# Pairing q, k blocks, moving DRAM copies and spreading branch loads in a one-layer encoder kernel

## The chip, the cores and the metric

The kernel runs on one core of a Trainium2 chip. The time is device microseconds of one launch; the number for a kernel is the median of its runs. A separate profiled execution gives the trace. Engines are called as in the profile: PE (TensorE, matmuls; PEld its weight loads), DVE (VectorE), ACT (ScalarE), POOL (GpSimd) and SP, whose queue issues most of the DMAs. Every engine takes its instructions in program order.

## The reference

One layer of a streaming encoder on x of 1024 tokens by 1024 features, all in f32:

```
h  = rmsnorm(x)
z  = h @ w_in                      # qa fa ia ga (4 x 512), qb kb vb (3 x 512), gate_a gate_b (2 x 1024)
oa = HGRN2(qa, fa, ia, ga)         # 4 heads of 128, chunk-wise linear recurrence
ob = BandAttn(qb, kb, vb)          # 8 heads of 64: q, k head-normalised; each chunk of 64 sees itself and 8 before it; bias by distance
x += (sigmoid(gate_a) * (oa @ w_branch_a) + sigmoid(gate_b) * (ob @ w_branch_b)) @ w_out
x += (silu(h2 @ w_gate) * (h2 @ w_up)) @ w_down          # h2 = rmsnorm(x)
x += sigmoid(h3 @ w_ple_gate) * (p @ w_ple_proj)         # h3 = rmsnorm(x)
```

## The kernel before

**Arithmetic.** Every f32 operand of a large matmul is split in two f32r parts: `hi`, a cast, and `lo = x - hi`. A product is three matmuls of 128x128 by 128x512 (hi hi, hi lo, lo hi). `gemm` issues them. A weight therefore costs a load into a raw tile, a cast on ACT and a subtraction on POOL before PE can use it.

**Order.** The program is written out as Python generators that are advanced in a fixed order, and `order` pins each engine to program order. A generator yields after a piece of work, usually six matmuls. `fetch` (L165) issues the load of the next weight of a planned list and appends a little generator to `self.later`; `tick` (L181) advances everything in `later` by one, so that the cast and subtraction of a weight are issued at the third tick after its fetch. The stream of q, k and branch work is wrapped in `ticked`, which ticks once per yield. There are four buffers for split weights (`RING`), two raw ones (`RAW`), 32 slots of 128x1024 f32 for everything large, and eight PSUM banks.

**Stages around the change.**
- *HGRN*: four heads, one after the other, in `hgrn_mix`. Seven levels per head (m = 1, 2, ..., 64) run mostly on DVE. They are woven with a fill of matmuls: two gate columns, then `attn_v` (v of the attention), then the first 20 yields of `attn_in`. At each level, and once more after the first output block, a head also calls `next(self.copies, None)`, which issues on SP one copy of 512 KB from a weight in DRAM to a scratch tile in DRAM. There are 32 of them (8 of w_out, 24 of w_down); later accumulating DMAs on POOL (`self.adds`) turn them into the sums of a Strassen product, one in each odd step of attention and more after it, first the eight of w_out.
- *q and k*: `attn_in` computes q, k for heads 0 to 3 and then 4 to 7 (`two`), eight blocks of 128 tokens each. Four weights, each two of eight feature chunks by 512 columns, make a set. `tokens` (L250) goes over the weights of a set and, for each, over the blocks of a group: one yield per weight and block. Here a group is a single block, 32 yields per set. The first group of a set takes its weights as they become ready (`lazy`); during the last block (b == 7) each of four yields fetches a weight of what comes next. `qk_norm` copies a block's q, k from PSUM to an SBUF tile, squares it into a second tile `sq`, and one tick later sums the squares on DVE, scales on POOL and, three ticks on, stores the block to DRAM.
- *attention*: `attention` runs 32 steps (pair of heads, block) and two more to drain, n = 0 to 33. For two = 0 the steps are blocks 0 to 7 with two pairs each (n = 0 to 15), then again for two = 1. Block b sees min(b + 1, 5) blocks of keys. A step takes two yields from `feed`, the rest of `attn_in` (44 yields; 4 ahead of step 0, done with step 19) and then `branch_a`. An even step loads the q, k block of the next even step (`qk_load`).
- *branch operands*: at the end of step 17 `keep_heads` stores the first two finished attention tiles, and `load_in(self.od)` loads the four HGRN outputs. `split_in` splits them (ACT cast, POOL subtraction) in steps 18, 19, 19 and 20 (`SPLITS`). `branch_a` (32 yields from step 20) multiplies them with four weights in turn, two output columns of blocks each, and gates the results; `branches` follows with the four weights of the other branch. `gate_load` loads two gate tiles per call.

The lines that are touched or followed: `FIRST` (L33), `hgrn_mix` (L526, L592), `attn_v` (L631), `qk_norm` (L650), `attn_in` (L669), `attention` (L808 to L850), `branch_a` (L1122), `branches` (L1147). The profile shows most instructions of DVE, ACT and POOL under L72, where a helper issues them, and all matmuls under L103 (transposes L106), so groups are told apart by tile names: `wr` raw weight, `wh` and `wl` its parts, `pm` a PSUM bank, `s` a slot, `m` a small tile, `d` a DRAM scratch tile.

Of the kernel before, what the change touches and what calls it, by code (L numbers as in the profile page):

```python
# [14 lines left out]
AF = mybir.ActivationFunctionType  # L15
# [15 lines left out]
SLOTS = 32  # L31
LATE = 8
FIRST = 5  # L33
RING = 4
RAW = 2
AHEAD = 3
# [38 lines left out]
class Trunk:  # L75
# [386 lines left out]
    def hgrn_mix(self, h):  # L462
# [26 lines left out]
        while m < P:  # L489
# [33 lines left out]
                    rows = slice(2 * m * j, 2 * m * j + m)  # L523
                    (self.V.tensor_copy if j == 0 else nc.scalar.copy)(av[rows, :, j, :], ps[rows, :8 * m].rearrange("p (c m) -> p c m", m=m))
            cur = nxt
            next(self.copies, None)  # L526
            if m == 2 and h < 3:
                next(more)
                self.head_load(h + 1)
# [97 lines left out]
    def attn_v(self):  # L627
        self.fetch()
        ws = []
        self.v = [self.slot() for _ in range(4)]  # L630
        for blks in ((0, 1), (2,), (3,), (4,), (5,), (6, 7)):  # L631
            pss = []
            for j, _ in enumerate(self.tokens(ws or self.lazy(ws), blks, pss)):
                if blks[0] == 0 and j == 1:
                    self.gate_keep()
                if blks[0] == 6 and j % 2:
                    self.fetch()
                yield 1296
            for b, ps in zip(blks, pss):
                for p in range(4):  # L640
                    self.nc.scalar.activation(self.v[p][:, b * P:b * P + P], ps[:, p * P:p * P + P], AF.Copy, scale=self.r[:, b:b + 1])
# [8 lines left out]
    def qk_norm(self, k, ps):  # L650

        late = self.stacks
        qk, sq = [self.small(HALF, tag="qk" if late else "bias", shape=(P, HALF if late else 640))[:, :HALF] for _ in range(2)]
        (self.V.tensor_copy if late else self.A.copy)(qk, ps)
        self.A.activation(sq, ps, AF.Square)
        yield
        ss = self.small(8)
        heads = lambda t: t.rearrange("p (a d) -> p a d", d=64)
        self.V.tensor_reduce(ss, heads(sq), axis=AX.X, op=ALU.add)
        b = k % 8  # L660
        self.V.tensor_scalar(ss, ss, 1.0 / 64, self.epsv[:, b:b + 1], ALU.mult, ALU.add)
        self.G.tensor_tensor(ss, ss, self.mhalf[:, 0:8], ALU.pow)
        self.G.tensor_tensor(heads(qk), heads(qk), ss[:, :].unsqueeze(2).to_broadcast([P, 8, 64]), ALU.mult)
        yield
        yield
        yield
        self.store(self.qk_at(k), qk)

    def attn_in(self):  # L669

        self.qkd = [self.spill() for _ in range(8)]
        for two in range(2):
            ws = []
            for b in range(8):
                pss = []
                for _ in self.tokens(ws or self.lazy(ws), (b,), pss):
                    if b == 7:
                        self.fetch()
                    yield 1296
                self.later.append(self.qk_norm(8 * two + b, pss[0]))  # L680

    def qk_load(self, k):
        if k < 16:
# [81 lines left out]
    def attention(self):  # L765
# [35 lines left out]
        for i in range(4):  # L801
# [3 lines left out]
            if i == 3:  # L805
                drain(stack(0))
                drain(self.hgrn_out())
        drain(self.copies)  # L808
        self.adds = chain(self.osum, self.wsum)
        while self.queue:  # L810
            self.rest()
# [2 lines left out]
        for n in range(whole + 2):  # L814
            if n % 2 and n < whole:
                next(self.adds)
            if n % 2 == 0:
                self.qk_load(n // 2 + 1)
            stage(n - 1, 1)
            next(feed, None)  # L820
            if n < whole:
                if steps[n][1] == 0:
                    self.ob.append(self.slot())
                scores(n)
            if n % 2:
                pv(n - 3)
                pv(n - 2)
            drain(stack(n + 1))
            for _ in range(SPLITS.count(n)):
                self.osrc.append(self.split_in(raws[len(self.osrc)]))  # L830
            if n in (whole - 4, whole - 3):
                bsrc.append(self.split_in(braws[len(bsrc)]))
            if n == whole:
                bsrc += [(self.slot(F32R), self.slot(F32R)) for _ in range(2)]
                self.split_half(bsrc, 0)
            next(feed, None)
            pt(n - 1, 1)
            stage(n, 0)
            stage(n, 1)
            pt(n - 1, 0)  # L840
            stage(n, 0)
            if n == 0:
                self.keep_heads(self.oa, self.od, self.done_heads)
            if n == whole // 2 + 1:
                self.keep_heads(self.ob, self.obd, [0, 1])
                raws = self.load_in(self.od)
            if n == whole // 2 + 4:
                for _ in range(2):
                    self.gate_load()
            if n == whole - 6:  # L850
                braws = self.load_in(self.obd[:2])
            yield 0
# [263 lines left out]
    def branch_a(self):  # L1116

        self.m = {}
        for dd in range(4):
            (w,) = self.got()  # L1120
            next(self.adds, None)
            if dd:  # L1122
                self.fetch()
            if dd < 2:
                self.gate_load()
            for i in range(2):
# [17 lines left out]
    def branches(self):  # L1144
        V = self.V
        gates, tile, src = self.bgates, self.branch_tile, self.bsrc
        drain(self.feed)  # L1147
        while self.later:
            self.tick()
# [1032 lines left out]
def drain(stream):  # L2182
    while True:
        try:
            next(stream)
        except StopIteration as e:
            return e.value
# [125 lines left out]
```

## Time and profile before

| | us |
|---|---|
| median of 3 runs | 1565.39 |
| lowest, highest | 1564.87, 1567.02 |
| profiled execution, its own time | 1567.15 |
| span of its trace | 1565.4 |

| engine | busy us | share of the span |
|---|---|---|
| PE | 1522.9 | 97% |
| PEld | 1253.3 | 80% |
| DVE | 1121.2 | 72% |
| POOL | 677.9 | 43% |
| ACT | 664.2 | 42% |

The mean granted clock of PE is 0.988. A line of the timeline reads: start, duration, engine, line, operation, written and read tiles, shapes, count, and in brackets the idle time of the engine before it with what ended that. In a table by stretches each row gives the stretch, its length, then busy time and instruction count of PE, PEld, DVE, ACT and POOL, then the granted clock, the share in which the DMA queues were busy, and GB/s. A line on DMA issues gives tiles, engine, operation, count, size and the median time from issue to landing.

### The profile page before, as it was taken

The numbers are of one execution on the slowest core, as the hardware profiler recorded it, in microseconds if no ns is written. First come the engines' busy times: TensorE is split into PE (matmuls) and PEld (weight loads), VectorE is DVE, ScalarE is ACT, GpSimd is POOL, SyncE is SP. The second block draws the span as 40 slices with busy tenths as digits, with TensorE's granted clock in tenths as the row PEclk, the third lists the DMA queues.
The fourth block names the chain that finished last, engine by engine and source line by source line (L and its number), as shares of the span: only waits on it lengthen the run. The fifth ranks groups of instructions, "written<-read, shape, count | busy, mean of one in ns | idle before, by whom it ended". The sixth has DMA issues, their size and how long they took to land.

```text
span 1565.4 us, 20771 instructions
## 1 busy us (share of the span) xinstructions
PE 1522.9 (97%) x7680; PEld 1253.3 (80%) x7680; DVE 1121.2 (72%) x1595; ACT 664.2 (42%) x1119; POOL 677.9 (43%) x382
## 2 busy tenths in 40 slices
PE   8999999999898996999999999999999999999998
PEld 6888888878686884888888788888888888888786
DVE  5876777476775666755988877777777756756668
ACT  6633333343335664651467322222222234446552
POOL 4233333320325327136210566665555544645445
PEclk9999999999999997999999999999999999999999
DMA  5543444588565448766354334443333288875325
GB/s 207 185 169 101 143 149 153 181 286 287 166 175 152 101 123 270 187 172 193 114 167 166 124 117 131 126 124 108 109 106 105 84 294 299 294 274 201 128 96 201
DMA packets 101940, 264.95 MB, mean 169 GB/s; under 512 B 10576, under 2 KB 15440, under 8 KB 101328
## 3 DMA queue, kind: packets, MB, share of 16 engines
q1 hardware_dynamic: 95296, 247.90, 45.5%
q0 software_dynamic: 6400, 15.73, 6.1%
q8 instruction: 60, 0.98, 0.3%
q14 instruction: 40, 0.33, 0.1%
q10 hardware_dynamic: 144, 0.02, 0.0%
HBM read 197.28 MB, written 97.78 MB: 188 GB/s over the span
## 4 chain that ended last, share of the span: by engine, by line
PE 66%; DVE 4%; DMA 3%; POOL 3%; issue 3%; ACT 1%; SPq 0%; POOLq 0%; ACTq 0%; DVEq 0%
PE pm L103 64%; DVE s L72 3%; PE pm L106 2%; DMA s<-d 1%; DMA d<-in_oq 1%; POOL wl L72 1%; POOL m L72 1%; POOL s L72 0%; POOL wl L151 0%; DMA wr<-in_wv 0%; DVE q L72 0%; DVE m L72 0%; POOL d L72 0%; DMA wr<-in_qk 0%; ACT wh L72 0%
## 5 line engine op out<-in xcount | busy, mean ns | idle before, releaser
L103 PE MATMUL pm<-s,whi 128*128 128x512 f32 x1904 | 586.4, 389 | 0.6 <-DVE t L72 0.6
L103 PE MATMUL pm<-s,wh 128*128 128x512 f32 (+1 forms) x1456 | 455.6, 394 | 10.6 <-ACT wh L143 5.2
L103 PEld LDWEIGHTS pm<-s,whi 128*128 128x128 f32 x1904 | 357.1, 188 | 75.4 <-DVE t L72 1.7
L103 PE MATMUL pm<-s,wlo 128*128 128x512 f32 x952 | 370.4, 389 | 0.0
L72 DVE TENSOR_TENSOR s<-s,s 128x512 f32<-128x512 f32 (+3 forms) x240 | 288.1, 1230 | 67.9 <-ACT s L72 53.7
L103 PEld LDWEIGHTS pm<-s,wh 128*128 128x128 f32 x1456 | 272.4, 189 | 69.9 <-ACT wh L143 5.2
L103 PE MATMUL pm<-s,wl 128*128 128x512 f32 (+1 forms) x728 | 284.8, 391 | 1.0 <-POOL wl L151 0.5
L151 POOL TENSOR_TENSOR wl<-wr,wh 128x1024 fp32r<-128x1024 f32 (+2 forms) x70 | 171.0, 2449 | 220.7 <-ACT wh L143 212.9
L72 DVE TENSOR_TENSOR t<-pm,t 128x512 f32<-128x512 f32 x168 | 115.7, 689 | 146.0 <-PE pm L103 123.3
L103 PEld LDWEIGHTS pm<-s,wlo 128*128 128x128 f32 x952 | 178.7, 188 | 37.5
L103 PE MATMUL pm<-wh,s 128*128 128x512 f32 x512 | 183.5, 414 | 0.7 <-ACT wh L72 0.7
L72 POOL TENSOR_TENSOR wlo<-q,whi 128x512 fp32r<-128x512 f32 x66 | 105.2, 1594 | 164.2 <-ACT whi L72 87.7
L72 POOL TENSOR_TENSOR wlo<-wr,whi 128x1024 fp32r<-128x1024 f32 (+1 forms) x67 | 139.8, 2092 | 69.7 <-ACT whi L72 60.6
L103 PEld LDWEIGHTS pm<-s,wl 128*128 128x128 f32 x728 | 137.5, 189 | 30.3 <-POOL wl L151 1.2
L143 ACT CAST wh<-wr 128x1024 fp32r<-128x1024 f32 (+3 forms) x81 | 80.1, 991 | 163.6 <-DMA wr<-d 47.6
L72 ACT CAST s<-s 128x1024 fp32r<-128x1024 f32 (+1 forms) x104 | 98.8, 970 | 66.5 <-DMA s<-d 32.5
L72 ACT CAST whi<-q 128x512 fp32r<-128x512 f32 (+1 forms) x99 | 75.0, 758 | 107.4 <-PE pm L103 87.1
L103 PEld LDWEIGHTS pm<-wh,s 128*128 128x128 f32 x512 | 98.7, 193 | 19.9 <-ACT wh L72 0.9
L72 POOL TENSOR_TENSOR s<-t,rb 128x512 f32<-128x512 f32 x44 | 70.6, 1606 | 98.4 <-ACT t L72 98.4
L103 PE MATMUL pm<-wl,s 128*128 128x512 f32 x256 | 102.8, 401 | 8.9 <-POOL wl L72 8.9
L72 POOL TENSOR_TENSOR wl<-wr,wh 128x1024 fp32r<-128x1024 f32 x25 | 62.8, 2534 | 83.7 <-ACT wh L72 71.7
L72 POOL TENSOR_TENSOR m<-m,mhalf 128x8 f32<-128x8 f32 (+1 forms) x24 | 35.5, 1480 | 139.0 <-DVE m L72 139.0
(149 smaller groups left out, 1808.3 us busy)
## 6 DMA issues: line engine op xcount, KB each, us to landing
s<-d SPq DMA_DIRECT2D x81, 512.0 KB, 7.0
d<-s SPq DMA_DIRECT2D x87, 256.0 KB, 2.3
wr<-d SPq DMA_DIRECT2D x36, 512.0 KB, 3.4
d<-s SPq DMA_DIRECT2D x30, 512.0 KB, 4.5
d<-t SPq DMA_DIRECT2D x54, 256.0 KB, 2.1
wr<-in_sz SPq DMA_DIRECT2D x24, 512.0 KB, 6.0
wr<-in_sg SPq DMA_DIRECT2D x22, 512.0 KB, 3.8
wr<-in_su SPq DMA_DIRECT2D x22, 512.0 KB, 4.1
```

What stands on the lines that cost most here:

```text
L72: return lambda *a, **k: self.trunk.order(op(*a, **k), self.key)
L103: return self.order(self.nc.tensor.matmul(*a, **k))
L106: return self.order(self.nc.tensor.transpose(*a, **k))
L143: self.nc.scalar.copy(hi[:, c], raw[:, c])
L151: rest.tensor_tensor(lo[:, c], raw[:, c], f32(hi[:, c]), ALU.subtract)
```

## The change

Seven edits:
1. `attn_in` takes its blocks in the groups (0, 1), 2, 3, 4, 5, (6, 7), like `attn_v` before it. A pair has two PSUM banks and eight yields. In the first set the four fetches fall on every second yield of the last pair.
2. In the second set the last pair fetches one weight (at its fourth yield), the first of branch a, instead of four.
3. `branch_a` fetches at the start of each of its four weights, not of the last three, and `branches` fetches one more, so that each weight is fetched about one weight ahead.
4. `qk_norm` squares in place in PSUM, and the sum of squares reads PSUM; the tile `sq` is gone.
5. The HGRN levels issue copies only at m = 2, 8 and 32 (and once after the first output block): 16 instead of 32.
6. The other 16 copies are issued in attention, two after the `qk_load` of each even step, until they are used up (step 14).
7. `load_in(self.od)` moves from the end of step 17 to the end of step 13.

```diff
+GROUPS = ((0, 1), (2,), (3,), (4,), (5,), (6, 7))
...
             cur = nxt
-            next(self.copies, None)
+            if m in (2, 8, 32):
+                next(self.copies, None)
...
-        qk, sq = [self.small(HALF, tag="qk" if late else "bias", shape=(P, HALF if late else 640))[:, :HALF] for _ in range(2)]
+        qk = self.small(HALF, tag="qk" if late else "bias", shape=(P, HALF if late else 640))[:, :HALF]
         (self.V.tensor_copy if late else self.A.copy)(qk, ps)
-        self.A.activation(sq, ps, AF.Square)
+        self.A.activation(ps, ps, AF.Square)
         yield
...
-        self.V.tensor_reduce(ss, heads(sq), axis=AX.X, op=ALU.add)
+        self.V.tensor_reduce(ss, heads(ps[:, :]), axis=AX.X, op=ALU.add)
...
-            for b in range(8):
+            for blks in GROUPS:
                 pss = []
-                for _ in self.tokens(ws or self.lazy(ws), (b,), pss):
-                    if b == 7:
+                for j, _ in enumerate(self.tokens(ws or self.lazy(ws), blks, pss)):
+                    if blks[0] == 6 and (j % 2 if two == 0 else j == 3):
                         self.fetch()
                     yield 1296
-                self.later.append(self.qk_norm(8 * two + b, pss[0]))
+                self.later += [self.qk_norm(8 * two + b, ps) for b, ps in zip(blks, pss)]
...
-        drain(self.copies)
         self.adds = chain(self.osum, self.wsum)
...
             if n % 2 == 0:
                 self.qk_load(n // 2 + 1)
+                next(self.copies, None)
+                next(self.copies, None)
...
             if n == whole // 2 + 1:
                 self.keep_heads(self.ob, self.obd, [0, 1])
+            if n == whole // 2 - 3:
                 raws = self.load_in(self.od)
...
             next(self.adds, None)
-            if dd:
-                self.fetch()
+            self.fetch()
...
         gates, tile, src = self.bgates, self.branch_tile, self.bsrc
+        next(self.feed, None)
+        self.fetch()
         drain(self.feed)
```

More of the change, by code (lines that the diff above doesn't have):

```diff
@@ L630, in attn_v @@
         self.v = [self.slot() for _ in range(4)]
-        for blks in ((0, 1), (2,), (3,), (4,), (5,), (6, 7)):
+        for blks in GROUPS:
             pss = []
@@ L673, in attn_in @@
             ws = []
-            for b in range(8):
+            for blks in GROUPS:
                 pss = []
-                for _ in self.tokens(ws or self.lazy(ws), (b,), pss):
-                    if b == 7:
+                for j, _ in enumerate(self.tokens(ws or self.lazy(ws), blks, pss)):
+                    if blks[0] == 6 and (j % 2 if two == 0 else j == 3):
                         self.fetch()
                     yield 1296
-                self.later.append(self.qk_norm(8 * two + b, pss[0]))
+                self.later += [self.qk_norm(8 * two + b, ps) for b, ps in zip(blks, pss)]
     def qk_load(self, k):
```

## The prediction

> **What bounds the kernel now.** I read the page first, for who is busy.
>
> ```profile
> span 1565.4 us, 20771 instructions
> ...
> PE 1522.9 (97%) x7680; PEld 1253.3 (80%) x7680; DVE 1121.2 (72%) x1595; ACT 664.2 (42%) x1119; POOL 677.9 (43%) x382
> ...
> PEclk9999999999999997999999999999999999999999
> ```
>
> TensorE (PE) is busy for 97%. The change removes no matmul, so it can only win back time in which PE stands still or runs at a lower clock. I then cut the part that the change touches (HGRN from 321 us, attention from about 468, the branches from about 690) into stretches.
>
> ```profile
> 345.00:358.00 13.00, 11.65 (x76) 10.18 (x75) 8.10 (x15) 4.13 (x12) 3.04 (x2) 1.00 0.96 307
> 358.00:395.00 37.00, 37.00 (x251) 31.63 (x250) 24.64 (x49) 14.09 (x37) 2.76 (x4) 1.00 0.81 272
> 395.00:432.00 37.00, 31.34 (x196) 25.40 (x195) 28.18 (x40) 14.87 (x32) 13.68 (x7) 0.91 0.52 164
> ...
> 486.00:506.00 20.00, 14.91 (x71) 10.27 (x70) 10.91 (x27) 12.34 (x35) 12.44 (x7) 0.83 0.65 159
> 506.00:580.00 74.00, 74.00 (x628) 61.07 (x628) 53.11 (x191) 50.50 (x128) 24.73 (x21) 1.00 0.45 103
> 580.00:622.00 42.00, 28.40 (x143) 19.50 (x138) 24.25 (x43) 20.29 (x54) 27.77 (x16) 0.76 0.80 247
> 622.00:693.00 71.00, 71.00 (x599) 59.01 (x599) 49.73 (x167) 49.25 (x117) 19.94 (x15) 1.00 0.64 162
> 693.00:745.00 52.00, 52.00 (x237) 42.99 (x234) 25.35 (x30) 9.96 (x12) 30.14 (x21) 1.00 0.69 232
> ```
>
> The columns are the stretch, its length, busy time (and instructions) of PE, weight load, DVE, ACT and POOL, the granted clock, the DMA share and GB/s. Four stretches lose time, their neighbours none. What each loses is its idle time plus what the lower clock takes, bounded by (1 - clock) times the busy time and times the whole length:
> - start, 345 to 358: 1.35 us idle
> - A, 395 to 432: 5.66 idle and 2.8 to 3.3 of clock, about 8.8
> - B, 486 to 506: 5.09 and 2.5 to 3.4, about 8.1
> - C, 580 to 622: 13.6 and 6.8 to 10.1, about 22
>
> Together some 40 us: no version of this change can win much more. The last row gives the unit of the sum: 52.00/237 = 0.219 us per 128x512 matmul, so one yield of the fill (six of them) is 1.32 us.
>
> **C, the branch operands and weights.**
>
> ```profile
> 581.83 3.40 SPq L98 DMA_DIRECT2D s<-d  x4
> ...
> 591.54 1.04 ACT L72 CAST s<-s 128x1024 fp32r<-128x1024 f32 x1 [4.99 <-DMA s<-d]
> ...
> 593.94 0.70 PE L103 MATMUL pm<-m,s 128*64 128x128 f32 x4 [4.62 <-ACT m L72]
> ...
> 600.77 5.15 POOL L72 TENSOR_TENSOR s<-s,s 128x1024 fp32r<-128x1024 f32 x2
> ...
> 603.52 8.28 DVE L72 TENSOR_SCALAR s<-s,m 128x256 f32<-128x256 f32 x1
> ...
> 605.42 2.82 POOL L72 TENSOR_TENSOR wl<-wr,wh 128x1024 fp32r<-128x1024 f32 x1
> ...
> 608.34 3.30 POOL L72 TENSOR_TENSOR wl<-wr,wh 128x1024 fp32r<-128x1024 f32 x1
> ...
> 611.95 0.66 PE L106 MATMUL pm<-eye,s 128*128 128x128 f32 x2 [3.60 <-DVE s L72]
> ...
> 614.60 2.35 POOL L72 TENSOR_TENSOR s<-s,s 128x1024 fp32r<-128x1024 f32 x1 [2.96 <-ACT s L72]
> ...
> 617.01 0.79 PE L103 MATMUL pm<-s,wh 128*128 128x512 f32 x1 [1.64 <-POOL s L72]
> ```
>
> Two things end waits here. First, the four operands are loaded at the end of step 17 (issued from 581.83) and cast at the head of step 18 (591.54). ACT takes its work in order, so the softmax behind the cast waits 4.99 us too, and PE 4.62. The change issues these loads at the end of step 13. Two steps take about 11.3 us:
>
> ```profile
> 512.48 0.32 SPq L98 DMA_DIRECT2D m<-d  x1
> ...
> 523.75 0.32 SPq L98 DMA_DIRECT2D m<-d  x1
> ```
>
> (one key-and-query load every second step), so the loads get over 20 us where they took 9.7, and this wait goes whole. At step 13 the 32 slots hold by my count 16 tiles of u, 4 of v, 4 of keys, 2 of ob: six are free, so the SP queue does not stop on a slot. In step 14 a key load and two copies are queued behind them on SP, needed ten microseconds later.
>
> Second, POOL forms in a row the lower parts of four operands (5.15 for two, 2.35 each) and four branch weights (2.8 to 3.3), and a 128x256 scaling on DVE takes 8.28 us, from 603.52 to 611.80, until POOL's run is over. PE waits 3.60 for it. The change keeps one branch weight here (fetched in step 17) and moves three to steps 20, 24 and 28. POOL is left with 9.85 for operands and 2.8 for the weight, beside the q, k scalings. What stays: in step 18 an operand and a weight back to back (2.35 + 2.8), in step 19 two operands (5.15), in step 20 one (2.35), 12.65 us in which DVE may be held. What a hold costs PE I take from two rows: 8.28 cost 3.60 (0.43), and under A two DVE operations that took 3.17 cost 1.48 (0.47). So 12.65 x 0.45 = 5.7 us of idling, and with the clock as in B (5.09 idle, some 3 more) 8 us. The bounds are 3 (each hold hidden) and 14 (each gets through to PE). I take 8, because both rows lie near 0.45. C gains 22 - 8 = 14.
>
> The trace shows the hold lasting over several POOL instructions. The Trainium skill ("SBUF — State Buffer", "SBUF: two separate sides") says that the port shared by DVE and POOL is an exclusive lock that whoever starts first keeps "for the whole instruction", that is one instruction; the 8.28 us row disagrees. What it would make of C is a rival below.
>
> **B, the second q, k weight set.**
>
> ```profile
> 487.30 0.60 ACT L72 ACTIVATE m<-pm 128x512 f32<-128x512 f32 x1 [3.17 <-DMA d<-m]
> ...
> 493.40 5.15 POOL L72 TENSOR_TENSOR wl<-wr,wh 128x1024 fp32r<-128x1024 f32 x2
> ...
> 496.29 0.79 PE L103 MATMUL pm<-wl,s 128*128 128x512 f32 x1 [3.66 <-POOL wl L72]
> ...
> 500.64 1.04 ACT L72 CAST wh<-wr 128x1024 fp32r<-128x1024 f32 x1 [5.46 <-DMA wr<-in_qk]
> ...
> 504.19 0.50 PE L103 MATMUL pm<-wl,s 128*128 128x512 f32 x1 [0.98 <-POOL wl L72]
> ```
>
> Before, the four weights of the next set are fetched in four successive yields (28 to 31) and needed in the next four (32 to 35). PE waits 3.66 and 0.98 for POOL, and ACT 5.46 for a load that could not start until POOL had freed one of two raw buffers. With blocks 6 and 7 as a pair the fetches fall on yields 25, 27, 29, 31, with 0 and 1 as a pair the needs on 32, 34, 36, 38: seven yields between, and one weight per step (2.6 us of POOL, 1.0 of ACT) instead of two. The 3.17 us that ACT waits before it can write sq (its buffer's last store is still going out) go with sq. I keep 2.6: a cast still stands one step behind its load, and in steps 0 and 2 two copies go ahead of it on SP. B gains 5.5.
>
> **A, the first q, k weight set, in HGRN.**
>
> ```profile
> 399.07 3.17 DVE L72 TENSOR_TENSOR s<-s,s 128x512 f32<-128x512 f32 x2
> ...
> 402.39 1.13 PE L103 MATMUL pm<-s,m 128*128 128x128 f32 x8 [1.48 <-ACT m L72]
> ...
> 414.74 0.50 PE L103 MATMUL pm<-wl,s 128*128 128x512 f32 x1 [0.60 <-POOL wl L72]
> ...
> 418.52 0.50 PE L103 MATMUL pm<-wh,s 128*128 128x512 f32 x1 [0.72 <-ACT wh L72]
> ...
> 421.38 0.79 PE L103 MATMUL pm<-wl,s 128*128 128x512 f32 x1 [2.36 <-POOL wl L72]
> ```
>
> Only the need changes here (attn_v fetches in pairs already): the third weight is first used two yields later, the fourth three. The waits of 0.60, 0.72 and 2.36 go, and with them most of the 3 us of clock. The 1.48 stays, and next is late the DVE chain of the HGRN levels (28.18 busy in 37), so I count 5 of 8.8.
>
> **Start, and half the copies.** 16 of 32 DRAM-to-DRAM copies leave HGRN, where DMA is at 0.81 to 0.96; the operand and weight loads land sooner. I count 0.5 of the 1.35 us. In attention they come two per even step up to step 14:
>
> ```profile
> d<-in_wq SPq DMA_DIRECT2D x20, 512.0 KB, 6.6
> wr<-in_qk SPq DMA_DIRECT2D x5, 512.0 KB, 8.1
> ```
>
> At the 307 GB/s of the start row a 512 KB copy is 1.7 us of all queues, two in 11.3 us raise the DMA share from 0.45 to about 0.75. They are issued behind the key load of their step, which is needed a step or more later. The adds that use them begin at step 17, three steps after the last. Cost: 0 to 3, I take 0.5.
>
> **The rest.** In place, Square writes PSUM and the reduction reads it:
>
> ```profile
> 498.64 0.68 DVE L72 COPY m<-pm 128x512 f32<-128x512 f32 x1
> ...
> 503.25 0.68 DVE L72 TENSOR_REDUCE m<-m 128x8 f32<-128x512 f32 x1
> ```
>
> A DVE pass over 512 columns is 0.68 from either memory, so 16 of them cost between -1 and +1, I take 0. A pair holds one PSUM bank more, and each bank until its reduction, a yield later. At most four of eight are then held while the scores want four: 0 to 5 us (0.5 in each of ten steps), I take 0.5, as the pairs of attn_v run in HGRN without a loss (358 to 395). In the branches the second to fourth weight come later. One weight feeds 48 matmuls, 10.5 us, which hides a load, a cast and 2.8 us on POOL; uncovered it would be a wait like the 3.66 above. I take 0.
>
> **Sum.** 14 + 5.5 + 5 + 0.5 - 1 = 24 us. The profiled execution took 1567.15 us (1565.4 of span, 1.75 around it), 1.76 over the median of 1565.39, and would come to 1543. For the median, 1541.
>
> **Rivals.**
> 1. C moves instead of shrinking. POOL's 12.65 us of operands and weight come with the scalings of blocks 6 and 7 and with DMA issues:
>
> ```profile
> 594.98 1.71 POOL L72 TENSOR_TENSOR m<-m,mhalf 128x8 f32<-128x8 f32 x1
> ...
> 596.77 1.03 POOL L72 TENSOR_TENSOR m<-m,m 128x512 f32<-128x512 f32 x1
> ...
> 597.76 1.12 POOL L72 DMA_DIRECT2D d<-in_wq  x1
> ```
>
> With two pairs of the first two and three of the last that is 21.5 us in steps 18 to 21, which take some 22: as full as before. The gate tiles loaded in step 20 are needed a step later, with no stall to cover them. Only the 4.62 us and some 3 of clock go, less 2.6 for the gates: C gains 5, the whole 15, 1550. For it: POOL was busy 27.77 of 42 us there. Against: three weights, 7 to 9 us, leave. Chance 0.2.
> 2. DVE gets the port between two POOL instructions. Holds of at most 2.35 us, three of them at 0.45, make 3.2 us, each too short to move the clock: C keeps 3, the gain is 29, 1536. For it: two more operands, split one by one in steps 28 and 29, and three weights lie in 622 to 693, where PE loses nothing. Against: the 8.28. Chance 0.15.
> 3. Slower: weights land later than a step after their issue, and ACT, in order, stops with them. Eight weights (four q, k, four of branch a) are cast one step, 5.6 us, behind the load. A landing takes 8.1 in HGRN, and if the copies and gates bring that to attention, each costs ACT 2.5, and PE with the clock twice that at worst: 20 to 40 us against 24, say 1571. It decides when a landing exceeds 5.6 us. Against: 8.1 was measured at a DMA share near 0.9, not 0.75. Chance 0.06.
> 4. Every stall that goes makes place for the next engine, DVE or POOL, and nothing is left: 1565. Chance 0.04.
>
> Rival 2 counts no clock since the start stretch idles 1.35 us at a clock of 1.00, while B and C, with single waits of 3.66 and more, show 0.83 and 0.76. The Trainium skill ("TensorE: Matmul & The Clock Gate", "What's actually happening") speaks of half clock after an idle window of about 3.4 us; the trace agrees in size.
>
> **Numbers.** The forecast has 0.55, with a range of its own of 1533 to 1549. With rivals 1 and 2 and the bounds (C keeping 3 to 14, banks and copies up to 8) the range is 1527 to 1556. A measurement of this kernel tells about 0.2%, 3 us. Faster 0.55 + 0.2 + 0.15 = 0.9, same 0.04, slower 0.06.
>
> **What would show it.** Right: no ACT wait on the s<-d loads; PE waits of under 2.5 us at both q, k set changes; one wl between the operand splits; a granted clock of 1.00 in all but C. Wrong: ACT waits on wr<-in_qk or wr<-in_ba of over 3 us, PE waits for DVE or ACT on PSUM banks in steps 4 to 9, or a DVE scaling that is held for 5 us or more in steps 18 to 21.

## The result, and the profile after

The changed kernel took 1552.82 us (median; 1551.46 to 1554.34), the kernel before 1565.13 us beside it. The ratio is 0.992, with a 95% interval of 0.9902 to 0.9937: faster, by 12.3 us. The forecast was 1541, with a range of 1527 to 1556. So the sign and the wide range held. The narrower 1533 to 1549, to which the forecast itself was given 0.55, did not, and the gain was half of the 24 us that were worked out. The profiled execution took 1554.34 us, 12.81 less than that of before; it is the highest of the four, 1.5 above the median, so the traces of other kernels can lie further from this one than their medians do.

The page of the kernel after, for the same rows that were read of before:

```profile
span 1552.5 us, 20777 instructions
...
PE 1518.9 (98%) x7680; PEld 1251.0 (81%) x7680; DVE 1122.6 (72%) x1594; ACT 665.0 (43%) x1119; POOL 683.2 (44%) x383
```

PE has the same 7680 matmuls and is busy 4 us less, since fewer of them ran at the lower clock; the rest of the gain is idle time. The stretches of the kernel after (same columns as before; B and C begin some microseconds earlier than they did). The kernel after has one line more at its head, so the helpers' lines are one higher (L73 for L72, L104 for L103):

```profile
345.00:358.00 13.00, 12.27 (x80) 10.66 (x79) 7.91 (x16) 3.96 (x11) 1.85 (x2) 1.00 0.50 175
...
395.00:432.00 37.00, 32.50 (x214) 27.31 (x213) 27.21 (x40) 15.91 (x35) 10.00 (x5) 0.95 0.52 154
432.00:468.00 36.00, 34.31 (x241) 28.94 (x240) 29.18 (x57) 10.44 (x25) 14.08 (x11) 1.00 0.46 148
478.00:506.00 28.00, 23.40 (x138) 16.94 (x138) 17.42 (x52) 17.50 (x54) 17.33 (x11) 0.94 0.93 290
...
580.00:612.00 32.00, 25.20 (x128) 17.83 (x126) 19.11 (x45) 18.86 (x52) 22.78 (x14) 0.84 0.81 240
```

A, B and C are all shorter and none is gone: the idle time is 4.50 in A, 4.60 in B and 6.80 us in C, and the clock is below 1.00 in each. To see where the 12.8 us came from, I took the same matmul in both traces, by its number on PE, and compared its start. Through A (from the matmul that began at 395 to the one that began at 432 before) 2.6 us were won; between 432 and 468 1.3 were lost; through B (468 to 512) 2.2 won; then 0.8 lost by 540; through C (575 to 622) 10.1 won. After that 1.0 lost and won back leaves 13.0 at the end. Gains of single stages below are counted in this way.

**A.** The first q, k set in the kernel after:

```profile
412.08 4.70 POOL L73 TENSOR_TENSOR wl<-wr,wh 128x1024 fp32r<-128x1024 f32 x2 [3.83 <-ACT wh L73]
412.36 1.06 ACT L73 CAST wh<-wr 128x1024 fp32r<-128x1024 f32 x1
...
415.05 2.88 DVE L73 TENSOR_TENSOR s<-s,s 128x512 f32<-128x512 f32 x2
...
418.08 1.53 PE L104 MATMUL pm<-s,s 128*64 128x64 f32 x16 [3.02 <-DVE s L73]
```

The three waits for a weight (0.60, 0.72, 2.36) are gone, as forecast. A new one of 3.02 us has come. The fourth weight's cast now runs at 412.36, ahead of a small copy of the HGRN scan that waits for DVE; before, it ran at 417.43, behind that copy. The copy is issued outside the helper that pins an engine's order (its line is L524, now L525), so it can change its place. Before and after:

```profile
417.04 0.36 ACT L524 COPY s<-pm 32x256 f32<-32x256 f32 x1 [4.33 <-DVE s L72]
417.43 1.04 ACT L72 CAST wh<-wr 128x1024 fp32r<-128x1024 f32 x1
```

```profile
418.44 0.36 ACT L525 COPY s<-pm 32x256 f32<-32x256 f32 x1 [4.50 <-DVE s L73]
```

So POOL subtracts the third and the fourth weight without a gap, the two DVE operations beside it take 2.88 us where they otherwise take 1.3, and PE waits for them.

**B.** The second set in the kernel after:

```profile
475.89 1.65 SPq L99 DMA_DIRECT2D wr<-in_qk  x1
...
483.02 1.05 ACT L73 CAST wh<-wr 128x1024 fp32r<-128x1024 f32 x1 [3.37 <-DMA wr<-in_qk]
...
486.64 0.33 PE L107 MATMUL pm<-eye,s 128*128 128x128 f32 x1 [2.42 <-DVE s L73]
...
493.50 1.05 ACT L73 CAST wh<-wr 128x1024 fp32r<-128x1024 f32 x1 [1.34 <-DMA wr<-in_qk]
```

The waits for POOL's weights (3.66, 0.98) and ACT's wait for the store are gone. The first load is issued at 475.89, ACT reaches its cast one step later and waits 3.37 us for it, and PE waits 2.42 us for work that stands behind it. The third cast waits 1.34. The DMA share of the stretch is 0.93, with moved copies in it.

**C.** The branch operands in the kernel after:

```profile
583.06 1.05 ACT L73 CAST s<-s 128x1024 fp32r<-128x1024 f32 x1
...
588.98 1.07 POOL L73 DMA_DIRECT2D d<-in_wq  x1
...
589.58 5.14 POOL L73 TENSOR_TENSOR s<-s,s 128x1024 fp32r<-128x1024 f32 x2
...
591.31 3.58 DVE L73 TENSOR_SCALAR s<-s,m 128x256 f32<-128x256 f32 x1
...
592.48 0.66 PE L104 MATMUL pm<-s,wh 128*128 128x512 f32 x1 [2.44 <-POOL s L73]
...
599.60 1.06 POOL L73 DMA_DIRECT2D d<-in_wq  x1 [4.87 <-DMA m<-d]
599.87 3.39 DVE L73 TENSOR_SCALAR s<-s,m 128x384 f32<-128x384 f32 x1
600.19 2.84 POOL L73 TENSOR_TENSOR s<-s,s 128x1024 fp32r<-128x1024 f32 x1
...
603.09 0.80 PE L104 MATMUL pm<-s,wh 128*128 128x512 f32 x1 [4.36 <-POOL s L73]
```

The cast waits for no load any more, so the 4.99 and 4.62 us are gone. PE now waits for the splits themselves, twice; the two waits, 2.44 and 4.36, are all of the stretch's 6.80 us of idle time. The second time POOL was not busy: it stood idle for 4.87 us in front of an accumulating DMA, with the last operand's split queued behind it. The DMA that it names, a key load, is not what held it: the accumulating DMA of 588.98 landed at 599.26, and the next went out 0.34 us after that. Two scalings on DVE are still held beside POOL (3.58 and 3.39 us), and PE waits for neither.

### The profile page after: what moved, and what is told of

The parts are those of the page before. It is cut to its first block, busy times and chain, and to the rows that moved or that the text cites. A ratio compares the mean times of both kernels' runs of the same rounds, so it can differ in the third digit from the quotient of the medians.

```text
span 1552.5 us, 20777 instructions
## 1 busy us (share of the span) xinstructions
PE 1518.9 (98%) x7680; PEld 1251.0 (81%) x7680; DVE 1122.6 (72%) x1594; ACT 665.0 (43%) x1119; POOL 683.2 (44%) x383
## 4 chain that ended last, share of the span: by engine, by line
PE 83%; DVE 8%; DMA 3%; issue 2%; POOL 2%; ACT 2%; SPq 0%; DVEq 0%; POOLq 0%; ACTq 0%
PE pm L104 81%; DVE s L73 6%; PE pm L107 3%; POOL s L73 1%; DMA wr<-in_qk 1%; ACT s L73 1%; DVE m L73 1%; DMA wr<-in_bb 1%; POOL wl L73 0%; DVE wl L152 0%; ACT wh L144 0%; DMA s<-in_x 0%; POOL wl L152 0%; DMA wr<-in_ow 0%; DMA m<-d 0%
## 5 line engine op out<-in xcount | busy, mean ns | idle before, releaser
L104 PE MATMUL pm<-s,whi 128*128 128x512 f32 x1904 | 586.4, 389 | 0.0
L104 PE MATMUL pm<-s,wh 128*128 128x512 f32 (+1 forms) x1456 | 455.1, 393 | 13.9 <-POOL s L73 6.8
L104 PEld LDWEIGHTS pm<-s,whi 128*128 128x128 f32 x1904 | 357.4, 188 | 74.2
L104 PE MATMUL pm<-s,wlo 128*128 128x512 f32 x952 | 370.6, 389 | 0.5 <-DVE wlo L73 0.5
L73 DVE TENSOR_TENSOR s<-s,s 128x512 f32<-128x512 f32 (+3 forms) x240 | 296.5, 1265 | 58.7 <-ACT s L73 42.5
L104 PEld LDWEIGHTS pm<-s,wh 128*128 128x128 f32 x1456 | 271.9, 189 | 72.7 <-POOL s L73 7.6
L104 PE MATMUL pm<-s,wl 128*128 128x512 f32 (+1 forms) x728 | 284.3, 391 | 0.5 <-POOL wl L152 0.5
L152 POOL TENSOR_TENSOR wl<-wr,wh 128x1024 fp32r<-128x1024 f32 (+3 forms) x71 | 177.0, 2496 | 218.7 <-ACT wh L144 215.3
L73 DVE TENSOR_TENSOR t<-pm,t 128x512 f32<-128x512 f32 x168 | 115.7, 689 | 147.3 <-PE pm L104 124.9
L104 PEld LDWEIGHTS pm<-s,wlo 128*128 128x128 f32 x952 | 178.7, 188 | 38.1 <-DVE wlo L73 1.2
L104 PE MATMUL pm<-wh,s 128*128 128x512 f32 x512 | 181.7, 410 | 0.0
L73 POOL TENSOR_TENSOR wlo<-q,whi 128x512 fp32r<-128x512 f32 x66 | 105.1, 1593 | 164.2 <-ACT whi L73 87.8
L73 POOL TENSOR_TENSOR wlo<-wr,whi 128x1024 fp32r<-128x1024 f32 (+1 forms) x67 | 139.8, 2093 | 68.4 <-ACT whi L73 59.3
L104 PEld LDWEIGHTS pm<-s,wl 128*128 128x128 f32 x728 | 137.5, 189 | 29.7 <-POOL wl L152 1.2
L144 ACT CAST wh<-wr 128x1024 fp32r<-128x1024 f32 (+2 forms) x82 | 81.2, 992 | 154.6 <-PE pm L104 41.2
L73 ACT CAST s<-s 128x1024 fp32r<-128x1024 f32 (+1 forms) x104 | 98.7, 970 | 61.7 <-DMA s<-d 27.0
L73 ACT CAST whi<-q 128x512 fp32r<-128x512 f32 (+1 forms) x99 | 75.0, 758 | 107.0 <-PE pm L104 87.1
L73 POOL TENSOR_TENSOR s<-t,rb 128x512 f32<-128x512 f32 x44 | 71.2, 1619 | 99.3 <-ACT t L73 99.3
L104 PEld LDWEIGHTS pm<-wh,s 128*128 128x128 f32 x512 | 97.5, 190 | 19.0
L104 PE MATMUL pm<-wl,s 128*128 128x512 f32 x256 | 101.0, 394 | 0.0
L73 POOL TENSOR_TENSOR wl<-wr,wh 128x1024 fp32r<-128x1024 f32 x25 | 61.0, 2444 | 90.3 <-ACT wh L73 83.5
L73 ACT ACTIVATE t<-s 128x512 f32<-128x512 f32 x44 | 27.8, 632 | 158.6 <-DVE s L73 154.6
```

Source lines behind the costliest of these rows:

```text
L73: return lambda *a, **k: self.trunk.order(op(*a, **k), self.key)
L104: return self.order(self.nc.tensor.matmul(*a, **k))
L144: self.nc.scalar.copy(hi[:, c], raw[:, c])
L152: rest.tensor_tensor(lo[:, c], raw[:, c], f32(hi[:, c]), ALU.subtract)
```

## The experiments

All ratios are to the kernel before, timed on the same chip, where its median was 1565 to 1567 us. The kernel after was not timed again beside the others, so a difference from it of under 3 us or so is not told by the times. The intervals of u_raws, u_weights, u_pairs and x_add overlap with that of the kernel after: for these the waits in the trace carry the argument. By the ratios u_raws is 2.7 and u_pairs 2.0 us above the kernel after, where the medians below have 3.8 for both.

| kernel | median us | ratio, 95% interval |
|---|---|---|
| after | 1552.82 | 0.992, 0.9902 to 0.9937 |
| u_copies | 1547.12 | 0.9877, 0.9861 to 0.9893 |
| u_raws | 1556.58 | 0.9937, 0.9923 to 0.9952 |
| u_weights | 1552.39 | 0.991, 0.9894 to 0.9925 |
| u_pairs | 1556.61 | 0.9933, 0.9919 to 0.9947 |
| x_add | 1549.31 | 0.9889, 0.9863 to 0.9915 |
| x_early | 1542.24 | 0.9845, 0.9822 to 0.9867 |
| x_splitdve | 1543.87 | 0.9853, 0.9831 to 0.9875 |
| x_tickp | 1544.09 | 0.9857, 0.9834 to 0.9881 |
| c_early_tick | 1537.97 | 0.9819, 0.9805 to 0.9833 |
| c_all | 1545.05 | 0.9864, 0.9848 to 0.988 |
| c_single | 1561.09 | 0.9967, 0.9955 to 0.998 |
| c_single2 | 1550.23 | 0.9896, 0.988 to 0.9913 |

### One part of the change undone

**u_copies**: all 32 copies in HGRN again, the rest as after.

```
-            if m in (2, 8, 32):
-                next(self.copies, None)
+            next(self.copies, None)
...
+        drain(self.copies)
         self.adds = chain(self.osum, self.wsum)
...
-                next(self.copies, None)
-                next(self.copies, None)
```

> The changed kernel with all 32 DRAM copies back in HGRN and none in attention. Theory (the move is a small gain in HGRN, paid back in part at the start of attention, where ACT waited 3.37 us for a q, k weight behind a full DMA): HGRN from 321 to 468 us loses 0.5 to 1.5 us again, the stretch around the second q, k set gains 2 to 4, the whole comes to 1550 to 1553 us. Rival (DMA load is what limits attention after the change): 1545 or less, with the ACT wait on the weight gone and the splits' stretch better too. Rival (the copies in HGRN were a main cost): 1558 or more.

It is 5.7 us faster than the kernel after, between what theory and rival gave: moving the copies cost time. C won 10.4 us here and 10.1 in the kernel after, so C does not pay for it. A and B do. In A:

```profile
412.16 2.38 POOL L73 TENSOR_TENSOR wl<-wr,wh 128x1024 fp32r<-128x1024 f32 x1 [3.83 <-ACT wh L73]
...
415.11 1.28 DVE L73 TENSOR_TENSOR s<-s,s 128x512 f32<-128x512 f32 x2
...
416.54 1.12 PE L104 MATMUL pm<-s,s 128*64 128x64 f32 x16 [1.41 <-DVE s L73]
...
417.28 1.05 ACT L73 CAST wh<-wr 128x1024 fp32r<-128x1024 f32 x1
```

The fourth cast is back behind the small copy, POOL does one weight at a time, DVE's pair takes 1.28 and PE waits 1.41 instead of 3.02. A wins 3.1 us more than in the kernel after: 1.6 of it is this wait, the rest is the lower clock, which does not come (1.00, after it had been 0.95). The wait itself is one of order on ACT and not of a transfer; that the moved copies turned the order is read from these traces, since no run moves the small copy alone. B won 2.8 us more, 1.7 of it again the clock:

```profile
478.00:506.00 28.00, 24.53 (x156) 17.99 (x154) 19.53 (x58) 20.25 (x59) 18.09 (x11) 1.00 0.64 178
...
479.72 1.05 ACT L73 CAST wh<-wr 128x1024 fp32r<-128x1024 f32 x1 [3.13 <-DMA wr<-in_qk]
...
487.59 1.05 ACT L73 CAST wh<-wr 128x1024 fp32r<-128x1024 f32 x1 [0.26 <-DMA wr<-in_qk]
```

The first cast waits as long as in the kernel after, so the copies do not make that wait. The third waits 0.26 and not 1.34, the DMA share is 0.64, and the clock stays at 1.00.

**u_raws**: the four operands loaded at the end of step 17 again.

```
-            if n == whole // 2 - 3:
                 raws = self.load_in(self.od)
```

> The changed kernel with the four branch operands loaded at the end of step 17 again, not of step 13. Theory (this edit is the largest part of the gain): the ACT wait of about 5 us on the operand load and the PE wait behind it come back, with a stretch of half clock; 1559 to 1562 us, 6 to 9 above the changed kernel. Rival (the fewer branch weights made the room, the load lands in time now): within 3 us of 1553.

```profile
587.76 1.04 ACT L73 CAST s<-s 128x1024 fp32r<-128x1024 f32 x1 [4.68 <-DMA s<-d]
...
591.11 0.69 PE L104 MATMUL pm<-m,s 128*64 128x128 f32 x4 [4.77 <-ACT m L73]
```

The wait is back in full (4.68 of ACT, 4.77 of PE). The time is 3.8 us above the kernel after by the medians, between theory (6 to 9) and rival (within 3), and the early loads are worth about that: in the trace C wins 4.5 us less than in the kernel after. C still wins 5.6 us of its 10.1 without them; which part brings these no run separates.

**u_weights**: all four branch weights fetched in the last pair, as before.

```
-                    if blks[0] == 6 and (j % 2 if two == 0 else j == 3):
+                    if blks[0] == 6 and j % 2:
...
-            self.fetch()
+            if dd:
+                self.fetch()
```

> The changed kernel with all four weights of branch a fetched in the last pair again (yields 1, 3, 5, 7 of it), and the branches' fetches as before. Theory (POOL orders the operand splits, and three more rests among them delay them): POOL busy from step 18 to 21 without a gap, PE waits for the splits grow by 3 to 6 us, 1556 to 1560 us. Rival (the weights were not in the way): within 2 us of 1553.

The same time as after, and C wins 10.3 us. Fetching the branch weights one by one brings nothing that these runs can tell.

**u_pairs**: single blocks in both sets, everything else as after.

```
-            for blks in GROUPS:
+            for blks in [(b,) for b in range(8)]:
...
-                    if blks[0] == 6 and (j % 2 if two == 0 else j == 3):
+                    if blks[0] == 7 and (two == 0 or j == 3):
```

> The changed kernel with single blocks in the q, k sets again (four fetches in the last block of the first set, one in that of the second), squares in place. Theory (the pairs remove waits for weights at both set changes, but a hold of DVE by POOL in HGRN and a wait of ACT for a load take most of it back): about 3 us above the changed kernel, 1554 to 1558, with PE waits for wl at both set changes. Rival (pairs hold too many PSUM banks): faster than 1552, with the PE waits on DVE in steps 4 to 9 gone.

It is 3.8 us above the kernel after by the medians, as the theory had it, but not for its reason: up to the end of the second set (575) the trace is only 1.1 us behind that of the kernel after. Of the waits of PE (total, times, longest):

```profile
PE pm L104 <- ACT wh L73: 8.6, 1, 8.6
```

The 8.6 is not in a q, k set: it is the first branch weight, which this version fetches in the last yield of the last single block, four yields later than in the pair. So this run does not measure pairs alone; c_single2 below says more.

### The waits that were left

**x_add**: the accumulating DMA that stood ahead of the last split is left to a later place.

```
-            next(self.adds, None)
+            if dd:
+                next(self.adds, None)
```

> The kernel after, but the accumulating transfer at the first weight of the branch product is left to a later place, so that it no longer stands on POOL ahead of the last operand's split. Theory (the accumulate, not issued before the one ahead of it has landed, holds POOL 4.87 us and with it the split, and the product waits 4.36 us for that): the second PE wait of the stage goes and most of its 6.8 us of half clock (3.4 us lost) with it; 1545 to 1548 us. The first wait, 2.44 us for the two splits of step 19, stays. Rival (the split is late for its own place in the order, the transfer only fills the time): the wait stays above 2.5 us, 1551 to 1553 us.

```profile
598.12 2.35 POOL L73 TENSOR_TENSOR s<-s,s 128x1024 fp32r<-128x1024 f32 x1 [3.52 <-ACT s L73]
...
600.52 0.50 PE L104 MATMUL pm<-s,wh 128*128 128x512 f32 x1 [1.93 <-POOL s L73]
```

The split starts 2.07 us sooner, as soon as ACT's cast is done, and the wait falls from 4.36 to 1.93. C wins 5.1 us more, the median 3.5. The mechanism holds; the gain stays short of the expectation, since the split stands late in the order even without the DMA ahead of it.

**x_early**: the operands split earlier.

```
-SPLITS = (18, 19, 19, 20)
+SPLITS = (15, 17, 17, 18)
```

> The kernel after, but the four operands are split behind steps 15, 17, 17 and 18 instead of 18, 19, 19 and 20. Theory (the loads, now issued at step 13, land in time for this, and only the splits' own late place on POOL is left of the stage's loss): both PE waits on a split go, 2.44 and 4.36 us, and their 10.2 us of half clock (5.1 us lost); less 1 us for a VectorE instruction held by two splits in a row, 1541 to 1544 us. Rival 1 (the loads, six gate tiles and copies share one queue, and the operands are not in at step 15): ScalarE waits for s<-d again, and the in-order engine delays attention itself: 1550 to 1556 us. Rival 2 (the splits only move their hold of VectorE into attention, 2.4 us for each of four): 1548 to 1551 us.

The C stretch and POOL in it:

```profile
580.00:612.00 32.00, 31.49 (x220) 24.01 (x220) 21.85 (x77) 24.89 (x73) 21.48 (x13) 1.00 0.88 254
```

```profile
580.00 7.10 POOL L73 TENSOR_TENSOR s<-s,s 128x1024 fp32r<-128x1024 f32 x3 [1.65 <-ACT s L73]
...
599.88 1.05 POOL L73 DMA_DIRECT2D d<-in_wq  x1 [9.36 <-issue]
```

PE has 31.49 of 32 us, at full clock. C wins 21.3 us, which is nearly all of the 22 that the prediction found in it. POOL now stands 9.36 us in front of the accumulating DMA, and it costs nothing because no split is behind it. The time is 10.6 us under that of after, as the theory had it.

**x_splitdve**: the four subtractions on DVE.

```
-        self.G.tensor_tensor(raw, f32(raw[:, :]), f32(hi[:, :]), ALU.subtract)
+        (self.V if len(self.osrc) < 4 else self.G).tensor_tensor(raw, f32(raw[:, :]), f32(hi[:, :]), ALU.subtract)
```

> The kernel after, but the subtraction of each of the four operand splits is done by VectorE instead of POOL. Theory (POOL's queue and its hold of VectorE are the price, the subtraction itself is cheap on VectorE, 2 x 0.65 us for 1024 columns by the 128x512 rows): both PE waits on a split go or fall below 1 us, 1542 to 1546 us. Rival (VectorE is as full there as POOL, its chain of softmax sums waits instead): waits on VectorE of 2 us or more in their place, 1549 to 1552 us.

```profile
587.79 2.36 DVE L73 TENSOR_TENSOR s<-s,s 128x1024 fp32r<-128x1024 f32 x2
```

1.18 us each on DVE, where POOL takes 2.4. The waits for the splits are gone and the time is 9.0 us under after. Some 1.5 us of it lie in A, ahead of all that this edit touches, where the clock happened to stay at 1.00 (see the last section). So two ways of getting the splits out of POOL's late queue bring about the same.

**x_tickp**: each fetched weight cast one step later, and the small copy pinned.

```
             def cast():
                 yield
                 yield
+                yield
...
-                    (self.V.tensor_copy if j == 0 else nc.scalar.copy)(av[rows, :, j, :], ...
+                    (self.V.tensor_copy if j == 0 else self.A.copy)(av[rows, :, j, :], ...
```

> The kernel after, with each fetched weight cast one step later, and ScalarE's small copy of the HGRN scan kept in written order, so that the fourth weight's cast comes behind it, as it did in the kernel before. Theory (at the first weight set two POOL subtractions back to back hold VectorE, 3.02 us of PE wait; at the second ScalarE waits 3.37 us at its cast for a load that landed 7 us after its issue, and PE waits 2.42 us behind it): both waits fall below 1.6 us and their half-clock stretches go; 1546 to 1549 us. Rival (the casts only move the wait to the weights' users, or to the next set): waits on wl or wh come back, 1552 to 1556 us.

```profile
395.00:432.00 37.00, 34.72 (x237) 29.43 (x236) 30.65 (x46) 17.04 (x36) 11.83 (x7) 1.00 0.50 154
...
478.00:506.00 28.00, 24.61 (x156) 17.74 (x154) 20.21 (x59) 19.86 (x56) 17.71 (x11) 1.00 1.02 301
```

A wins 6.3 us and B 5.9, both at full clock, although the DMA share in B is higher than ever. In A the 3.02 became 1.47, in B the wait of 2.42 is gone. C won 4.8 more as well, which was not aimed at; 3.1 of that is clock. In all 8.7 us under after, better than expected.

### The repairs together

**c_early_tick**: x_early and x_tickp in one.

> The kernel after with both repairs: operands split behind steps 15, 17, 17 and 18, and weights cast one step later with ScalarE's small copy in written order. Theory (the losses that were left in the branch stage and at the two weight sets are independent): their gains against the kernel after add up, 10.6 us and 8.7 us, to 1533 to 1536 us. Rival (they share a cause, the transfers' queue or the place of the clock's windows): 1538 to 1542 us, not below the better of the two by more than 3 us.

1537.97 us, the fastest of all, 14.9 under the kernel after and 28 under before (0.9819, 0.9805 to 0.9833). That lies between theory and rival.

```profile
395.00:432.00 37.00, 34.74 (x237) 29.45 (x236) 30.55 (x47) 17.03 (x36) 11.92 (x7) 1.00 0.51 158
...
478.00:506.00 28.00, 24.44 (x154) 17.86 (x153) 19.42 (x56) 19.24 (x56) 18.42 (x12) 1.00 1.02 304
...
580.00:612.00 32.00, 30.58 (x220) 23.65 (x220) 25.62 (x78) 22.36 (x62) 17.15 (x12) 1.00 0.95 278
```

A, B and C have full clock. The gains of 10.6 and 8.7 do not quite add: x_tickp had 4.8 of its gain in C, which x_early wins too, and 10.6 + 8.7 - 4.8 = 14.5 is near the 14.9 that came.

**c_all**: c_early_tick, with the copies back in HGRN as in u_copies.

> As the run with both repairs, and all 32 copies back in the HGRN, as before the change. Theory (moving the copies cost 5.7 us only because it turned ScalarE's order at the first set and because the weights of the second were cast before they had landed): with both repaired, the same time as with both repairs alone, within 1.5 us. Rival (the copies cost time of their own in attention, through the transfers they delay): 3 us or more faster than with both repairs alone.

It went the other way from both: 7.1 us slower than c_early_tick. The loss is early in HGRN:

```profile
347.79 1.04 ACT L73 CAST wh<-wr 128x1024 fp32r<-128x1024 f32 x1 [4.79 <-DMA wr<-in_wv]
...
348.89 0.50 PE L104 MATMUL pm<-wh,s 128*128 128x512 f32 x1 [2.70 <-ACT wh L73]
```

A weight of `attn_v` is cast at 347.79, where c_early_tick casts it at 343.54, and it has to wait for its load. That load goes out on SP at 340.22; in c_early_tick, with half the copies on the queue, it went out at 337.10, and in u_copies, with all of them but the casts a step sooner, at 337.31, and PE waits for it in neither. So it takes the copies and the late casts together. 6 us are lost between 321 and 358, 3.4 of them by the clock. The moved copies have no single price: moving them lost 5.7 us in one company and won 7.1 in another.

**c_single** and **c_single2**: single blocks, once with both repairs and once with x_early's alone (the diff of u_pairs on each).

> As the run with both repairs, but the q, k blocks run one by one in both sets, as before the change. Theory (pairs are worth the 10.5 us that were forecast, of which the kernel after shows only half since other waits took their place): 1543 to 1547 us, 8 us or more above the run with both repairs. Rival (pairs are worth about the 4 us that undoing them alone showed): 1537 to 1540 us.

> The kernel after with the early operand splits alone (so that the branch stage no longer waits), its weights cast as in the kernel after, and the q, k blocks one by one: against the run with early splits and pairs, 1542.24 us, this is the pairs' worth with nothing else moved. Theory (in the kernel after pairs bring little, since the hold by two POOL subtractions and the wait for the cast take their place; undoing them cost 1.1 us up to the end of the second set): 1543 to 1547 us. Rival (the full 10.5 us that were forecast for both sets): 1551 to 1554 us.

c_single is 23.1 us above c_early_tick:

```profile
PE pm L104 <- POOL wl L73: 17.6, 6, 5.8
```

So it does not measure pairs: with single blocks and weights cast a step later PE waits for these, six times, which is the price of the two edits together. c_single2 against x_early is cleaner: 8.0 us. Up to the end of the second set (575) only 1.5 us of that have come, as the theory had it. The rest arises in C, and not from q and k:

```profile
593.52 1.04 ACT L73 CAST wh<-wr 128x1024 fp32r<-128x1024 f32 x1
...
594.61 0.90 PE L104 MATMUL pm<-s,wh 128*128 128x512 f32 x2 [3.99 <-ACT wh L73]
```

The cast of a branch weight runs at 593.52, in x_early at 583.73, and PE waits 3.99 us for it. So the time was nearer to the rival, and the reason was neither: undoing the pairs also put the fetch of the first branch weight four yields later.

## Why the prediction was right, and why its sizes were not

**Start.** Forecast 0.5 of gain. The DMA share fell from 0.96 to 0.50, and the 1.35 us wait for wl went. What stands in its place is a wait for DVE of 0.73. By 395 the kernel is 0.24 us ahead of the one before (0.65 won in this stretch, the rest lost earlier). Right within its size.

**A.** Forecast 5, measured 2.6. The three waits went as said. The step that failed is "and with them most of the 3 us of clock", with the DVE chain as what is late next: that chain was not late by its own work, but through two POOL subtractions back to back, at 3.02 us of PE and a clock of 0.95 (some 1.8 of 37 us). The prediction took ACT's order around the set as fixed. With the old order back (u_copies) A wins 5.7, with the copy pinned and the casts a step later (x_tickp, c_early_tick) 6.3.

**B.** Forecast 5.5, measured 2.2. The waits that were to go went. The term "I keep 2.6" for a cast one step behind its load was too small: the wait for it is 2.42, but the stretch idles 4.60 and runs at a clock of 0.94 (1.7 us of 28), so that some 6 were kept. With the cast a step later B wins 5.9.

**C.** Forecast 14, measured 10.1. Right: the loads' wait goes whole, and u_raws brings it back. The term "C keeps 8" was too small; it kept 12 (6.80 idle and 5 of clock). The step that failed is how holds reach PE. The prediction priced 12.65 us of POOL work through DVE, at 0.45. In the trace PE waits for the splits directly, 2.44 and 4.36, because `branch_a` multiplies with them from step 20 on, and the second is doubled by an accumulating DMA in front of it that no step of the prediction looked at. The holds that it did price cost PE nothing (3.58 and 3.39 us on DVE, no wait of PE for either), so that 8 and 12 are of one size is luck. The other reason given for C, that three branch weights leave POOL, was worth nothing (u_weights).

**Copies.** Forecast a cost of 0.5, within 0 to 3. Measured 5.7, out of the bounds. The bounds were made from the key loads of attention. The price came from A, by the turn of ACT's order, and from B, where the third weight landed later. Of the 5.9 us that A and B gave up against u_copies, some 3.4 are the lower clock, which came in both.

**Pairs.** Forecast a cost of 0.5 for PSUM banks, measured 2.1 (1.3 between 432 and 468, 0.8 between 512 and 540). The single-block runs u_pairs and c_single2 lose neither. The first is not a bank. Two blocks' sums of squares come to DVE together, and the HGRN chain behind them is late:

```profile
439.66 0.66 DVE L73 TENSOR_REDUCE m<-pm 128x8 f32<-128x512 f32 x1
...
440.50 0.68 DVE L73 TENSOR_REDUCE m<-pm 128x8 f32<-128x512 f32 x1
...
442.80 1.13 PE L104 MATMUL pm<-s,m 128*128 128x128 f32 x8 [1.28 <-ACT m L73]
```

Before, the wait at this place was 0.43. The cause of the second stays open: the longest wait of PE there is 0.24. Against what A and B won, this leaves little for the pairs: undoing them costs 1.1 us (u_pairs) and 1.5 (c_single2) up to 575, where A and B had been forecast to win 10.5. The reduction takes the 0.68 us from PSUM that was taken from SBUF, so the term of 0 for the edit in place was right.

**Rest of the branches.** Forecast 0; no wait for a branch weight or a gate tile is in the trace after. Right.

**Sum.** 14 + 5.5 + 5 + 0.5 - 1 = 24 became 10.1 + 2.2 + 2.6 + 0.2 - 2.1 = 13.0. The part of the sum that was wrong is what stays behind when a wait goes. That the time still fell into 1527 to 1556 owes as much to the width of the range as to the sum; its lower end does not even follow from its terms, which allow 30 us at most (C keeping 3, no cost for copies and banks), 1535. Of the signs listed, two came (no wait of ACT on s<-d, one wl between the splits); the clock stayed below 1.00 in A and B, PE waited 3.02 at the first set, and ACT waited 3.37 for wr<-in_qk, which was listed as a sign of being wrong.

**Rivals.** Rival 1 named the nearest time, 1550, and the right place, POOL in steps 18 to 21. Its mechanism was only half of it: POOL was not full but idle in front of a DMA, and the gates cost nothing. Rival 2 (no long holds) is what x_early shows: with the splits earlier, scalings on DVE beside three POOL subtractions in a row take 0.46 and 1.09 us (128 and 256 columns), where one took 8.28 before and two took 3.58 and 3.39 in the kernel after. What decides between a long and a short hold is open. Rival 3's mechanism appeared in B, where the load issued at 475.89 was waited for until 483.02; it cost PE 2.42 us and not 20. Rival 4 is out.

## What to carry to other kernels

When a wait goes, look at what the consumer of that result needs next and from which queue: here the operands were loaded four steps sooner and were still split at the old place, and moving the splits too was worth nearly as much again. Look through each in-order queue ahead of an instruction that has become critical, DMA issues included, since a transfer that cannot go out yet holds all that is behind it. Undoing one part of a change does not measure that part when another part was fitted to it (the pairs, the late casts and the copies each showed another price in each company).

## What the runs showed of the hardware

**An accumulating DMA holds POOL.** The 512 KB accumulates from a weight in DRAM were never two in flight at once in the traces of before and after. Twice before and four times after, one came close behind another and went out some 0.3 us after the other had landed (599.26 and 599.60 above). POOL stood idle for it, here after an issue at 508.45 that landed at 516.28:

```profile
516.60 1.06 POOL L73 DMA_DIRECT2D d<-in_oq  x1 [7.04 <-issue]
```

They write different tiles, so the data do not ask for it; what makes the second wait, no run separates. Accumulates from one scratch tile in DRAM to another do overlap, two at a time: one that would have been the third in flight stood 4.97 us and went out at 618.05, 0.32 us after another had landed. The profile names another DMA, or "issue", as the cause.

**The lower clock depends on where a wait falls.** The same wait of 3.02 us in A gave a clock of 0.95 in the kernel after, and no lower clock in x_splitdve:

```profile
417.35 1.12 PE L104 MATMUL pm<-s,s 128*64 128x64 f32 x16 [3.02 <-DVE s L73]
```

```profile
395.00:432.00 37.00, 32.50 (x228) 27.64 (x227) 27.92 (x43) 17.05 (x36) 9.67 (x5) 1.00 0.48 149
```

The idle time is equal (32.50 busy of 37 in both), but 16 matmuls took 1.53 us there and 1.12 here. The Trainium skill ("TensorE: Matmul & The Clock Gate", "What's actually happening") says that the clock's window runs freely and does not start with the work; these two rows agree. A stretch of half clock lasts 3.41 us or a multiple of it in these traces. In the kernel after one runs from 418.6 to 422.0, and in the 3.41 us ahead of that PE was busy for 0.51. In x_splitdve the next fall of the clock is at 497.7; counted back from there in steps of 3.41 us, the wait falls across two steps (from 412.37 and from 415.78), and PE was busy for 1.96 and 1.85 in them. Nor does it take a wait of the whole 3.41 us: the fall in B, at 486.8, came behind one of 2.42, with PE busy for 0.98 of the 3.40 us ahead. So a shift of everything upstream can bring a slow stretch or take one away, and 1.7 us, half of such a stretch, can come or go with an edit that is elsewhere. The kernel after has one that before has not, with hardly any idle time around it; what brought that one is open:

```profile
825.00:850.00 25.00, 24.74 (x119) 20.81 (x118) 21.11 (x25) 18.56 (x29) 4.61 (x3) 0.93 0.54 182
```
